# Handling of the samples' columns and the written order of VectorE and ScalarE in the RMS norms of a five-stage transformer step

## The chip, the cores and the metric

The kernel runs on one core of a Trainium2 chip. A core has TensorE (PE in the profile, PEld for its weight loads), VectorE (DVE), ScalarE (ACT), GpSimd (POOL) and SyncE (SP, which only issues transfers). The metric is the device time of one launch in microseconds. All arithmetic is fp32 in and out; the matrix products use pairs of rounded values (hi and lo), as told below.

## What is computed

The reference takes 1024 prompt columns and 64 sample columns (8 sequences of 8 tokens) of 1024 features. Four stages run one after the other: attention (stage 0), a gated MLP (stage 1), an RWKV mixing layer (stage 2) and another MLP (stage 3), then a last norm. Each stage starts with an RMS norm whose output is modulated:

```
r  = 1 / sqrt(mean(x*x over features) + eps)
h  = x * r * scale[stage] + shift[stage]
x  = x + gate[stage] * block(h)
```

The factors scale, shift and gate belong to a condition: the prompt has one condition for all its columns, and each of the 8 sample sequences has its own. So for the prompt they are one number a feature, for the samples 8 numbers a feature.

## The kernel before

Features lie on the partitions: x is eight tiles f = 0 to 7 of 128 features. The 1088 columns are worked in two halves: A has 576 prompt columns (products in chunks of 288), B has 448 prompt columns and the 64 samples (one chunk of 512). So the samples are columns 448 to 511 of a B half; an A half has none. Each half runs each stage's norm, so there are ten norms with the last ones.

A norm has three steps. `rms` (L246) squares x on ScalarE (sq, L253), sums over partitions by TensorE (ssq, L255), takes a square root on ScalarE (rv, L259), refines it in six VectorE operations (L260 to L265), spreads the result over all partitions by four TensorE products, one for each quarter of the columns (rb, L269), and copies them alternately by ScalarE (L120) and VectorE (L122) into R. `norm_split` (L294) then makes for each f the modulated tile hf and its rounded parts hhi and hlo: for the prompt, VectorE multiplies (L279), ScalarE adds the shift and rounds (L304), VectorE takes the rest (L305). For the samples `modulate` has POOL multiply by R (L283), by the scales (L284) and add the shifts (L285), ScalarE rounds (cast, L120) and POOL takes the rest (L292). `rw_norm` does the same for stage 2, where the modulated tile is kept (h) and mixed with its neighbour column (x, L828) before it is split into xhi and xlo.

`dense` (L329) runs over output tiles m. For each it loads a weight tile (wst), which `weight` (L313) rounds to wh on ScalarE (L323), the rest wl half on POOL (L325) and half on VectorE (L326). Then for each f it multiplies wh·hi (L339), wh·lo (L340) and wl·hi (L341) into one output tile dq. Three such tiles can be open at a time, so TensorE uses each hi and lo part up to three times before it has to wait for the next f. `residual` (L345) takes dq back into x: for the prompt one VectorE operation (L354); for the samples VectorE multiplies by the gates (rs, L357) and POOL adds (L360).

Other work runs beside the dense products: attention (softmax-like scans L529, products with the running result L530) beside stages 0 and 1, RWKV's chains (S, L1137; lane work tm and lxn, L1191 and L1193; qc, L1300 and on) beside stages 1 to 3. Code order gives each engine's instructions only loosely: a scheduler at build time decides by its own costs the order in which each engine runs them, and on the chip every engine keeps to that order and waits where an operand is late. Weight transfers are issued on SP (L320).

Of the kernel before, what the change touches and what calls it, by code (L numbers as in the profile page):

```python
# [10 lines left out]
F32 = mybir.dt.float32  # L11
# [44 lines left out]
SLOT = 576  # L56


C_ID, C_SEL9, C_SELB, C_MN, C_M64, C_M8, C_BLK, C_B8 = 0, 128, 144, 656, 664, 792, 920, 1048
C_H16, C_SELN, C_MQ, C_MQ1, C_MN1 = 1056, 1072, 1200, 1264, 1328  # L60
C_N = 1336


def make_consts():
    c = np.zeros((128, C_N), np.float32)
    p = np.arange(128)
    c[:, C_ID:C_ID + 128] = np.eye(128)
    for v in range(9):
        c[p % 32 == v, C_SEL9 + v] = 1.0
    for g in range(4):  # L70
        c[32 * g, C_SELB + 128 * g:C_SELB + 128 * (g + 1)] = 1.0
    for t in range(8):
        c[p % 8 > t, C_MN + t] = 1.0
    s = (p % 64)[:, None]
    t = np.arange(64)[None, :]
    c[:, C_M64:C_M64 + 64] = s < t
    c[:, C_M64 + 64:C_M64 + 128] = s <= t
    same = (s // 8) == (t // 8)
    c[:, C_M8:C_M8 + 64] = (s < t) & same
    c[:, C_M8 + 64:C_M8 + 128] = (s <= t) & same  # L80
    c[:64, C_BLK:C_BLK + 64] = 1.0
    c[64:, C_BLK + 64:C_BLK + 128] = 1.0
    for b in range(8):
        c[(p % 64) // 8 == b, C_B8 + b] = 1.0
    for h in range(16):
        c[p // 8 == h, C_H16 + h] = 1.0
    c[:, C_MQ:C_MQ + 64] = t < s
    c[:, C_MQ1:C_MQ1 + 64] = t >= s
    c[:, C_MN1:C_MN1 + 8] = 1.0 - c[:, C_MN:C_MN + 8]
    c[p % 32 == 0, C_SELN:C_SELN + 64] = 1.0  # L90
    c[p % 32 == 16, C_SELN + 64:C_SELN + 128] = 1.0
    return c


class Kern:
# [35 lines left out]
    def setup(self, ctx):  # L131
# [12 lines left out]
        self.beside(iter(()), 0.0)  # L144
        self.eps = self.misc.tile([128, 1], F32, name="eps")
        nc.vector.memset(self.eps, EPS)

    def load_params(self):

# [96 lines left out]
    def rms(self, x, pt, tmp, ps, tag, slot, rslot=None):  # L246

        nc = self.nc
        W, w = pt.W, pt.W // 4
        q = ps.tile([128, 512], F32, tag=tag, name="ssq")  # L250
        for f in range(NT):
            sq = tmp.tile([128, W], F32, tag=slot, name="sq")
            nc.scalar.activation(sq, x[f], AF.Square)  # L253
# [12 lines left out]
        R = tmp.tile([128, W], F32, tag=rslot or slot, name="R", bufs=2 if rslot else None)  # L266
        for g in range(4):
            qb = ps.tile([128, 512], F32, tag=tag, name="rb")
            nc.tensor.matmul(qb[:, :w], self.cst[:, C_SELB + 128 * g:C_SELB + 128 * g + 128], r,  # L269
                             start=True, stop=True)  # L270
            self.copy(R[:, w * g:w * g + w], qb[:, :w])
        return R

    def modulate(self, s, f, x, R, pt, t):

        nc = self.nc
        mod = self.mod[s]
        P, S = slice(0, pt.NP), slice(pt.NP, pt.W)
        nc.vector.scalar_tensor_tensor(t[:, P], x[f][:, P], mod[:, 8 + f, 0:1], R[:, P], ALU.mult,  # L279
                                       ALU.mult)  # L280
        if pt.NP < pt.W:
            ts = t[:, S].rearrange("p (b t) -> p b t", b=8)
            nc.gpsimd.tensor_mul(t[:, S], x[f][:, S], R[:, S])  # L283
            nc.gpsimd.tensor_mul(ts, ts, mod[:, 8 + f, 1:9].unsqueeze(2).to_broadcast([128, 8, 8]))  # L284
            nc.gpsimd.tensor_add(ts, ts, mod[:, f, 1:9].unsqueeze(2).to_broadcast([128, 8, 8]))  # L285
        return mod[:, f, 0:1]

    def split(self, src, hi, lo, heng="a", leng="v"):
        nc = self.nc
# [4 lines left out]
    def norm_split(self, s, x, R, pt, pool, tmp, slot):  # L294

        nc = self.nc
        hi, lo = [], []
        P, S = slice(0, pt.NP), slice(pt.NP, pt.W)
        for f in range(NT):
            t = tmp.tile([128, pt.W], F32, tag=slot, name="hf")  # L300
            B = self.modulate(s, f, x, R, pt, t)
            a = pool.tile([128, pt.W], F32R, tag="h", name="hhi")
            b = pool.tile([128, pt.W], F32R, tag="h", name="hlo")
            nc.scalar.activation(a[:, P], t[:, P], AF.Identity, bias=B)  # L304
            nc.vector.scalar_tensor_tensor(b[:, P], t[:, P], B, a[:, P].bitcast(F32), ALU.add,  # L305
                                           ALU.subtract)
            if pt.NP < pt.W:
                self.split(t[:, S], a[:, S], b[:, S], "a", "g")
            hi.append(a)
            lo.append(b)  # L310
        return hi, lo


# [31 lines left out]
    def residual(self, s, x, pt, tmp):  # L345
# [4 lines left out]
        def evac(m, c0, n, q):  # L350
# [4 lines left out]
            if np_ < n:  # L355
# [1 line left out]
                nc.vector.tensor_mul(t, q[:, np_:n].rearrange("p (b t) -> p b t", b=8),  # L357
                                     mod[:, 16 + m, 1:9].unsqueeze(2).to_broadcast([128, 8, 8]))
                xv = x[m][:, pt.NP:].rearrange("p (b t) -> p b t", b=8)
                nc.gpsimd.tensor_add(xv, xv, t)  # L360
        return evac


# [495 lines left out]
    def rw_norm(self, x, R, pt, pool, tmp):  # L859
# [2 lines left out]
        e = 1 if pt.o else 0  # L862
        W = pt.W
        hi, lo, hs = [], [], []

        def mixed(f):
            t = tmp.tile([128, W], F32, tag="n", name="x")
# [5 lines left out]
        for f in range(NT):  # L873
# [4 lines left out]
                nc.gpsimd.tensor_copy(he[:, 0:1], self.hl[:, f:f + 1])  # L878
            B = self.modulate(2, f, x, R, pt, h)
            nc.scalar.activation(h[:, :pt.NP], h[:, :pt.NP], AF.Identity, bias=B)  # L880
            if not e:
                nc.gpsimd.tensor_copy(self.hl[:, f:f + 1], h[:, W - 1:W])
            nc.sync.dma_start(self.hscr[f][:, pt.cols], h)
# [877 lines left out]
```

## Time and profile before

| | before |
|---|---|
| median of 3 runs | 3700.04 us (3698.4 to 3703.11) |
| profiled execution | 3712.77 us, its span 3710.8 us |
| TensorE busy | 3497.1 us, 94% |
| VectorE / ScalarE / POOL busy | 63% / 43% / 33% |
| mean granted TensorE clock | 0.962 |

The columns of a timeline row are: start, length, engine, line, operation, output and input, count, and in brackets the engine's idle time before it with what ended it. A waits row has total us, times and the longest. A group of a tile has the shortest, median and longest duration in ns. The profiled execution is 12.7 us longer than the median, so a sum worked out in it is applied as a difference.

### The profile page before, as it was taken

To read this page: it belongs to the slowest core of one execution; us is meant where nothing else is said; L and a number is where in the kernel's file an instruction comes from. 1 tells how busy PE (TensorE), PEld (TensorE's weight loads), DVE (VectorE), ACT (ScalarE), POOL (GpSimd) and SP (SyncE) were. 2 spreads that over 40 slices of the span, in tenths; PEclk is the share of its full clock that TensorE was granted. 3 is DMA by queue.
4 is the path that set the end of the run, shared out by engine and by line. 5 is a ranking of instruction groups with operands and counts; after the bars stand their busy time and mean duration, and the time that the engine had idled before them with its cause. 6 is when DMAs were issued, how large, how long until landed. Compare 5 with 4: busy or idle time off the path is not lost.

```text
span 3710.8 us, 72191 instructions
## 1 busy us (share of the span) xinstructions
PE 3497.1 (94%) x26360; PEld 2785.7 (75%) x26360; DVE 2320.9 (63%) x4718; ACT 1594.7 (43%) x3342; POOL 1235.3 (33%) x1692
## 2 busy tenths in 40 slices
PE   8999999899999999988799998998899999989998
PEld 5786767688888877766677776656698888877887
DVE  4246778996555556687846556666884666645444
ACT  3145666764333345634334445543433344332232
POOL 1136544443222222223423234223221222243332
PEclk9999999999999999988899998998899999989999
DMA  8845444125989885666254445557344444333332
GB/s 303 278 153 185 155 132 114 46 74 201 333 318 346 310 315 163 198 202 202 80 148 138 122 146 160 192 175 228 115 134 132 143 140 139 99 113 111 97 94 83
DMA packets 431860, 632.43 MB, mean 170 GB/s; under 512 B 144209, under 2 KB 244434, under 8 KB 431506
## 3 DMA queue, kind: packets, MB, share of 16 engines
q1 hardware_dynamic: 368242, 530.80, 44.5%
q10 hardware_dynamic: 63264, 97.02, 7.8%
q8 instruction: 209, 3.42, 0.4%
q14 instruction: 145, 1.19, 0.1%
HBM read 521.66 MB, written 106.01 MB: 169 GB/s over the span
## 4 chain that ended last, share of the span: by engine, by line
PE 40%; DVE 7%; DMA 3%; issue 2%; POOL 1%; ACT 1%; SPq 1%; ACTq 0%; DVEq 0%; POOLq 0%
PE dq L339 11%; PE dq L340 11%; PE dq L341 10%; DVE lxn L1193 1%; DVE tm L1191 1%; PE qc L1310 1%; PE qc L1300 1%; PE qc L1319 1%; PE yq L1467 1%; PE bonq L1459 0%; PE qc L1314 0%; PE invq L1260 0%; DMA s_v<-vt 0%; DVE wl L326 0%; PE qc L1323 0%
## 5 line engine op out<-in xcount | busy, mean ns | idle before, releaser
L325 POOL TENSOR_TENSOR wl<-wst,wh 128x256 fp32r<-128x256 f32 (+1 forms) x512 | 648.0, 1267 | 1580.3 <-ACT wh L323 1367.6
L323 ACT CAST wh<-wst 128x512 fp32r<-128x512 f32 (+1 forms) x512 | 424.7, 834 | 747.2 <-PE dq L340 589.9
L339 PE MATMUL dq<-hhi,wh 128*128 128x288 f32 (+1 forms) x2112 | 712.7, 338 | 31.2 <-ACT hhi L120 24.5
L340 PE MATMUL dq<-hlo,wh 128*128 128x288 f32 (+1 forms) x2112 | 709.0, 336 | 3.3 <-POOL prod L525 1.4
L341 PE MATMUL dq<-hhi,wl 128*128 128x288 f32 (+1 forms) x2112 | 704.6, 334 | 1.5 <-POOL wl L325 1.5
L326 DVE TENSOR_TENSOR wl<-wst,wh 128x256 fp32r<-128x256 f32 (+1 forms) x512 | 353.8, 694 | 264.6 <-ACT wh L323 226.2
L339 PE MATMUL dq<-uh,wh 128*128 128x288 f32 (+1 forms) x1536 | 505.7, 334 | 4.0 <-DVE rs L357 1.7
L340 PE MATMUL dq<-ul,wh 128*128 128x288 f32 (+1 forms) x1536 | 507.2, 331 | 0.0
L341 PE MATMUL dq<-uh,wl 128*128 128x288 f32 (+1 forms) x1536 | 505.3, 332 | 0.0
L339 PEld LDWEIGHTS dq<-hhi,wh 128*128 128x128 f32 x2112 | 402.8, 191 | 78.1 <-ACT hhi L120 25.5
L340 PEld LDWEIGHTS dq<-hlo,wh 128*128 128x128 f32 x2112 | 402.1, 190 | 51.0 <-issue 14.7
L341 PEld LDWEIGHTS dq<-hhi,wl 128*128 128x128 f32 x2112 | 401.7, 190 | 45.3 <-issue 14.5
L354 DVE SCALAR_TENSOR_TENSOR x<-dq,mod,x 128x288 f32<-128x288 f32 (+1 forms) x432 | 245.3, 569 | 269.9 <-PE dq L341 267.3
L339 PEld LDWEIGHTS dq<-uh,wh 128*128 128x128 f32 x1536 | 287.7, 188 | 43.5 <-issue 11.7
L529 DVE TENSOR_TENSOR_SCAN prod<-prod 128x256 f32<-128x256 f32 (+5 forms) x264 | 247.4, 938 | 104.9 <-ACT prod L520 65.3
L340 PEld LDWEIGHTS dq<-ul,wh 128*128 128x128 f32 x1536 | 288.4, 188 | 30.6 <-issue 9.2
L341 PEld LDWEIGHTS dq<-uh,wl 128*128 128x128 f32 x1536 | 288.1, 188 | 29.5 <-issue 7.0
L339 PE MATMUL dq<-xhi,wh 128*128 128x288 f32 (+1 forms) x576 | 206.4, 359 | 2.6 <-DVE gt L122 1.1
L340 PE MATMUL dq<-xlo,wh 128*128 128x288 f32 (+1 forms) x576 | 201.8, 350 | 3.0 <-POOL xlo L292 1.6
L341 PE MATMUL dq<-xhi,wl 128*128 128x288 f32 (+1 forms) x576 | 199.2, 346 | 0.0
L451 DVE TENSOR_TENSOR ut<-ut 128x288 f32<-128x288 f32 (+1 forms) x192 | 153.1, 798 | 40.5 <-ACT ut L450 37.8
L453 ACT CAST uh<-ut 128x288 fp32r<-128x288 f32 (+1 forms) x192 | 95.2, 496 | 189.2 <-DVE ut L451 186.8
(300 smaller groups left out, 6296.6 us busy)
## 6 DMA issues: line engine op xcount, KB each, us to landing
pagek<-cache_kT SPq DMA_DIRECT2D x128, 512.0 KB
pagev<-cache_v SPq DMA_DIRECT2D x128, 512.0 KB
adaw<-ada_w SPq DMA_DIRECT2D x192, 256.0 KB
wst<-w_up SPq DMA_DIRECT2D x96, 512.0 KB
wst<-w_down SPq DMA_DIRECT2D x192, 256.0 KB
st<-s_st SPq DMA_DIRECT2D x40, 672.0 KB
wst<-sb_w_qkv SPq DMA_DIRECT2D x48, 512.0 KB
wst<-w_up ACTq DMA_DIRECT2D x32, 512.0 KB
```

The lines of the kernel that those rows point to most:

```text
L323: nc.scalar.copy(wh, st)
L325: nc.gpsimd.tensor_sub(wl[:, :h], st[:, :h], wh[:, :h].bitcast(F32))
L326: nc.vector.tensor_sub(wl[:, h:], st[:, h:], wh[:, h:].bitcast(F32))
L339: nc.tensor.matmul(q, wh[:, k, :], h, start=k == 0, stop=False)
L340: nc.tensor.matmul(q, wh[:, k, :], l, start=False, stop=False)
L341: nc.tensor.matmul(q, wl[:, k, :], h, start=False, stop=k == kt - 1)
L354: nc.vector.scalar_tensor_tensor(xs, q[:, :np_], g, xs, ALU.mult, ALU.add)
L451: nc.vector.tensor_mul(t[:, :n], t[:, :n], t[:, :n])
L453: nc.scalar.copy(a, t[:, :n])
L529: nc.vector.tensor_tensor_scan(r, r, r, 1.0 if carry is None else carry, ALU.mult, ALU.bypass)
L1191: eng.tensor_mul(t, lt[P, s, s + 1:32].unsqueeze(2).to_broadcast([N, a, c]), xn[P, s, 0:c].unsqueeze(1).to_broadcast([N, a, c]))
L1193: eng.tensor_add(xn[P, s + 1:32, 0:c], xn[P, s + 1:32, 0:c], t)
```

## The change

Five edits.

1. The samples of all eight f are modulated together on VectorE: `modulate_samples` makes one tile hs (128 x 8 x 64), by eight multiplications with R and then one multiplication and one addition over all 512 values, with scales and shifts broadcast. ScalarE still rounds them; VectorE takes the rest (L314 of the new kernel).
2. The samples' residual add moves from POOL to VectorE (L380).
3. The four rb products use only 32 rows each, the row group in which the quarter's result stands (`self.R4[g]`), and the table of constants is smaller by 384 columns.
4. `rms` begins with a square root of a small tile into a tile `warm`.
5. `norm_split` runs under a manual schedule for VectorE and ScalarE: their instructions keep the order written there, hf0, hf1, lo0, hf2, lo1 and so on. Other work may still be put between them.

```diff
+        nc.scalar.activation(self.warm, self.eps, AF.Sqrt)
...
-            nc.tensor.matmul(qb[:, :w], self.cst[:, C_SELB + 128 * g:C_SELB + 128 * g + 128], r,
-                             start=True, stop=True)
+            rows = self.R4[g]
+            nc.tensor.matmul(qb[:, :w], self.cst[rows, C_SELB:C_SELB + 128], r[rows], start=True,
+                             stop=True)
...
-        if pt.NP < pt.W:
-            ts = t[:, S].rearrange("p (b t) -> p b t", b=8)
-            nc.gpsimd.tensor_mul(t[:, S], x[f][:, S], R[:, S])
-            nc.gpsimd.tensor_mul(ts, ts, mod[:, 8 + f, 1:9].unsqueeze(2).to_broadcast([128, 8, 8]))
-            nc.gpsimd.tensor_add(ts, ts, mod[:, f, 1:9].unsqueeze(2).to_broadcast([128, 8, 8]))
...
+    def modulate_samples(self, s, x, R, pt, tmp, slot):
+
+        nc = self.nc
+        mod = self.mod[s]
+        S = slice(pt.NP, pt.W)
+        t = tmp.tile([128, NT, TS], F32, tag=slot, name="hs")
+        for f in range(NT):
+            nc.vector.tensor_mul(t[:, f, :], x[f][:, S], R[:, S])
+        v = t.rearrange("p f (b t) -> p f b t", b=8)
+        for op, j in ((ALU.mult, 8), (ALU.add, 0)):
+            nc.vector.tensor_tensor(v, v, mod[:, j:j + NT, 1:9].unsqueeze(3).to_broadcast(
+                [128, NT, 8, 8]), op)
+        return t
...
+        def lower(f, B):
+            nc.vector.scalar_tensor_tensor(lo[f][:, P], ts[f][:, P], B, hi[f][:, P].bitcast(F32),
+                                           ALU.add, ALU.subtract)
             if pt.NP < pt.W:
-                self.split(t[:, S], a[:, S], b[:, S], "a", "g")
+                nc.vector.tensor_sub(lo[f][:, S], hs[:, f, :], hi[f][:, S].bitcast(F32))
+        with self.tc.manual_schedule(engines={mybir.EngineType.DVE, mybir.EngineType.Activation}):
+            if pt.NP < pt.W:
+                hs = self.modulate_samples(s, x, R, pt, tmp, slot)
+            last = None
+            for f in range(NT):
...
+                nc.scalar.activation(hi[f][:, P], ts[f][:, P], AF.Identity, bias=B)
+                if pt.NP < pt.W:
+                    nc.scalar.copy(hi[f][:, S], hs[:, f, :])
+                if last:
+                    lower(*last)
+                last = f, B
+            lower(*last)
...
-                nc.gpsimd.tensor_add(xv, xv, t)
+                nc.vector.tensor_add(xv, xv, t)
```

In `rw_norm` the samples' h is likewise copied by ScalarE out of an hs tile. The new kernel's line numbers are 1 higher in `rms` and about 20 higher behind `norm_split`.

What this does to the order of the instructions is shown at three places. The first is VectorE at the norm of stage 3's B half, before (x, dq, rs: the residual; ssq, rv, R: the norm; mod: the table of scales, shifts and gates):

```order
L357 TENSOR_TENSOR rs<-dq,mod_1507 128x64
L326 TENSOR_TENSOR wl<-wst,wh 128x512
L260 TENSOR_SCALAR rv<-ssq 128x128
...
L122 COPY R<-rb 128x128 x2
L279 SCALAR_TENSOR_TENSOR hf<-x,mod_3223,R 128x448 x6
L305 SCALAR_TENSOR_TENSOR hlo<-hf,mod_3223,hhi 128x448 x5
L279 SCALAR_TENSOR_TENSOR hf<-x,mod_3223,R 128x448 x2
L305 SCALAR_TENSOR_TENSOR hlo<-hf,mod_3223,hhi 128x448 x3
```

and in the changed kernel:

```order
L377 TENSOR_TENSOR rs<-dq,mod_1513 128x64
L346 TENSOR_TENSOR wl<-wst,wh 128x512
L380 TENSOR_TENSOR x<-x,rs 128x64
L261 TENSOR_SCALAR rv<-ssq 128x128
...
L121 COPY R<-rb 128x128 x2
L291 TENSOR_TENSOR hs<-x,R 128x64 x8
L294 TENSOR_TENSOR hs<-hs,mod_3219 128x512 x2
L280 SCALAR_TENSOR_TENSOR hf<-x,mod_3219,R 128x448 x2
L311 SCALAR_TENSOR_TENSOR hlo<-hf,mod_3219,hhi 128x448
L314 TENSOR_TENSOR hlo<-hs,hhi 128x64
L280 SCALAR_TENSOR_TENSOR hf<-x,mod_3219,R 128x448
```

The residual add and ten operations on hs are new on this engine, and each lo follows the next f's hf, where six hf ran ahead of the first lo.

The second is VectorE at the same norm of stage 1, where RWKV's lane operations (tm, lxn) stand beside it. Before:

```order
L357 TENSOR_TENSOR rs<-dq,mod_179 128x64
L326 TENSOR_TENSOR wl<-wst,wh 128x512
L1137 TENSOR_TENSOR S<-s_20900,cst 64x192
...
L265 TENSOR_TENSOR rv<-rv 128x128
L1191 TENSOR_TENSOR tm<-llt,lxn 72x31
L122 COPY R<-rb 128x128
...
L122 COPY R<-rb 128x128
L1191 TENSOR_TENSOR tm<-llt,lxn 72x87
L279 SCALAR_TENSOR_TENSOR hf<-x,mod_828,R 128x448 x3
L1193 TENSOR_TENSOR lxn<-lxn,tm 72x29x3
L279 SCALAR_TENSOR_TENSOR hf<-x,mod_828,R 128x448 x3
```

and in the changed kernel:

```order
L377 TENSOR_TENSOR rs<-dq,mod_181 128x64
L1215 TENSOR_TENSOR tm<-llt,lxn 72x112
L346 TENSOR_TENSOR wl<-wst,wh 128x512
L380 TENSOR_TENSOR x<-x,rs 128x64
...
L266 TENSOR_TENSOR rv<-rv 128x128
L1215 TENSOR_TENSOR tm<-llt,lxn 72x207
...
L291 TENSOR_TENSOR hs<-x,R 128x64 x5
L1215 TENSOR_TENSOR tm<-llt,lxn 72x240
L291 TENSOR_TENSOR hs<-x,R 128x64 x3
L1217 TENSOR_TENSOR lxn<-lxn,tm 72x20x12
L294 TENSOR_TENSOR hs<-hs,mod_834 128x512
```

The twelve S operations between the last residual and rv have gone ahead of the residual, with the TensorE products that they feed, and lane operations stand between the steps of the norm instead.

The third is ScalarE's start, in the changed kernel:

```order
L251 ACT_TABLE_LOAD
L251 ACTIVATE warm<-eps 128x1 x10
L164 ACT_TABLE_LOAD
L164 ACTIVATE cs<-c 128x72
L254 ACTIVATE sq<-x 128x576 x8
L260 ACT_TABLE_LOAD
L260 ACTIVATE rv<-ssq,eps 128x144
```

All ten warm-up square roots, one written at each norm, stand ahead of the first operation of the program, and the first norm still has a table load before its square root. At stage 1's A half (mixed with attention), the stretch of VectorE from the first hf to the last lo holds 11 rows of attention before and 25 in the changed kernel: 10 scans (5 before), 9 products L550 (5), two copies (1) and four casts (none).

More of the change, by code (lines that the diff above doesn't have):

```diff
@@ L69, in make_consts @@
         c[p % 32 == v, C_SEL9 + v] = 1.0
-    for g in range(4):
-        c[32 * g, C_SELB + 128 * g:C_SELB + 128 * (g + 1)] = 1.0
+    c[p % 32 == 0, C_SELB:C_SELB + 128] = 1.0
     for t in range(8):
@@ L146, in setup @@
         nc.vector.memset(self.eps, EPS)
+        self.warm = self.misc.tile([128, 1], F32, name="warm")
     def load_params(self):
```

34 lines of the change are left out of this document (16 added, 18 removed).

## The prediction

> **What bounds the kernel now.** I read the share of busy time first, then the list of waits, and then the timeline around each norm. The page's first part:
>
> ```profile
> PE 3497.1 (94%) x26360; PEld 2785.7 (75%) x26360; DVE 2320.9 (63%) x4718; ACT 1594.7 (43%) x3342; POOL 1235.3 (33%) x1692
> ```
>
> TensorE is busy for 94% of the span, so an edit pays only where TensorE stands still. The change touches no matmul of the dense products; it can only shorten the stalls of TensorE around the ten norms, or lengthen them. The waits that name its lines (total us, times, longest):
>
> ```profile
> ACT sq L253 <- POOL x L360: 41.5, 22, 5.0
> PE dq L339 <- ACT hhi L120: 24.5, 3, 10.5
> ```
>
> The second row is the target: three times, once in each norm_split of a B half, TensorE waits for the cast of the samples' columns, 24.5 us together. The first is ScalarE waiting for the add of the samples; ScalarE is 43% busy, and this matters only where squares of a norm are the last thing TensorE waits for. The norm of stage 3's B half shows the chain whole:
>
> ```profile
> 3312.01 0.69 DVE L354 SCALAR_TENSOR_TENSOR x<-dq,mod,x 128x448 f32<-128x448 f32 x1 [3.85 <-PE dq L341]
> 3312.61 0.21 DVE L357 TENSOR_TENSOR rs<-dq,mod 128x64 f32<-128x64 f32 x1
> 3312.90 0.69 DVE L326 TENSOR_TENSOR wl<-wst,wh 128x512 fp32r<-128x512 f32 x1
> 3313.00 1.72 POOL L325 TENSOR_TENSOR wl<-wst,wh 128x512 fp32r<-128x512 f32 x1 [3.41 <-ACT wh L323]
> 3314.68 0.31 POOL L360 TENSOR_TENSOR x<-x,rs 128x64 f32<-128x64 f32 x1
> 3315.03 0.63 ACT L253 ACTIVATE sq<-x 128x512 f32<-128x512 f32 x1 [1.62 <-POOL x L360]
> ...
> 3319.21 2.04 PE L269 MATMUL rb<-rv,cst 128*128 128x128 f32 x8 [2.98 <-DVE rv L265]
> ...
> 3321.29 0.29 DVE L122 COPY R<-rb 128x128 f32<-128x128 f32 x1 [0.56 <-PE rb L269]
> 3321.66 3.61 POOL L283 TENSOR_TENSOR hf<-x,R 128x64 f32<-128x64 f32 x6 [6.67 <-DVE R L122]
> 3321.69 4.07 DVE L279 SCALAR_TENSOR_TENSOR hf<-x,mod,R 128x448 f32<-128x448 f32 x6
> 3322.50 2.64 ACT L304 ACTIVATE hhi<-hf,mod 128x448 fp32r<-128x448 f32 x4 [1.37 <-DVE hf L279]
> 3325.24 3.47 POOL L284 TENSOR_TENSOR hf<-hf,mod 128x64 f32<-128x64 f32 x6
> 3328.67 2.01 POOL L285 TENSOR_TENSOR hf<-hf,mod 128x64 f32<-128x64 f32 x6
> 3328.99 0.24 ACT L120 CAST hhi<-hf 128x64 fp32r<-128x64 f32 x1 [3.85 <-POOL hf L285]
> ...
> 3329.29 0.80 PE L339 MATMUL dq<-hhi,wh 128*128 128x512 f32 x1 [8.03 <-ACT hhi L120]
> 3331.01 0.79 PE L340 MATMUL dq<-hlo,wh 128*128 128x512 f32 x1 [0.93 <-POOL hlo L292]
> ```
>
> R is complete at 3321.58. The prompt's first hi part is there 1.6 us later, yet the first product starts at 3329.29, because POOL runs all its first multiplications, then all second ones, and only then an addition that a cast can use. The groups of the tile hf (duration in ns: shortest, median, longest):
>
> ```profile
> L305 DVE SCALAR_TENSOR_TENSOR hlo<-hf,mod,hhi x48: 653/786/873, 24.2 to 3335.8; 128x576 fp32r<-128x576 f32 x24, 128x448 fp32r<-128x448 f32 x24
> L283 POOL TENSOR_TENSOR hf<-x,R x24: 309/695/4675, 280.9 to 3333.2; 128x64 f32<-128x64 f32 x24
> L284 POOL TENSOR_TENSOR hf<-hf,mod x24: 288/382/942, 284.0 to 3334.3; 128x64 f32<-128x64 f32 x24
> L285 POOL TENSOR_TENSOR hf<-hf,mod x24: 284/290/2307, 287.1 to 3334.8; 128x64 f32<-128x64 f32 x24
> ```
>
> The profiled execution took 3712.77 us, 12.7 above the median of 3700.04. My sum is a difference worked out inside the profiled execution; I take it from the median.
>
> **Norm of stage 3, B half.** Removed: the add on POOL behind its 1.72-us weight part. On DVE the add stands behind L326, which ends at 3313.59; at about the 0.21 us of L357 it is done at 3313.8, not 3314.99: −1.2. From there to R nothing changes but the four rb matmuls, now on 32 rows each. No row has this form. They cost at most the 2.04 us they take now; four copies on two engines (0.29 each) follow in any case, so the gain is 0 to 0.8, and I take 0.5. R is then complete at about 3319.9. Next on DVE come eight 128x64 multiplications at 0.2 (the 0.21 of L357) and two 128x512 operations at 0.69 (L326), 3.0 us; the first hf of 0.68 (4.07/6), its hi of 0.66 (2.64/4) and the cast of 0.24: the first product at about 3324.5, not 3329.29, −4.8. The lo parts follow on DVE, 0.65 and 0.2 each, faster than TensorE asks, so the 0.93 wait for POOL's lo goes too. Some of this returns later, since stage 3's first weights and the final norm of the A half follow. I take **−5**, bounds −7 to −2.
>
> **Norm of stage 1, B half.** Same chain, with RWKV lane work in it:
>
> ```profile
> 1788.00:1814.00 26.00, 8.41 (x75) 6.45 (x76) 16.00 (x42) 9.83 (x23) 10.46 (x18) 0.61 0.36 108
> ```
>
> This row is a window: PE, PEld, DVE, ACT, POOL busy. TensorE works 8.41 of 26 us.
>
> ```profile
> 1788.76 0.65 DVE L354 SCALAR_TENSOR_TENSOR x<-dq,mod,x 128x448 f32<-128x448 f32 x1
> ...
> 1796.84 1.28 ACT L259 ACT_TABLE_LOAD   x1
> 1798.13 0.37 ACT L259 ACTIVATE rv<-ssq,eps 128x128 f32<-128x128 f32 x1
> ...
> 1802.95 0.19 DVE L1191 TENSOR_TENSOR tm<-llt,lxn 72x31 f32<-72x31 f32 x1 [2.03 <-DMA llt<-s_l]
> ...
> 1803.88 0.28 DVE L122 COPY R<-rb 128x128 f32<-128x128 f32 x1
> ...
> 1804.23 7.21 POOL L283 TENSOR_TENSOR hf<-x,R 128x64 f32<-128x64 f32 x6 [13.92 <-DVE R L122]
> ...
> 1813.55 1.65 PE L339 MATMUL dq<-hhi,wh 128*128 128x512 f32 x3 [10.50 <-ACT hhi L120]
> ```
>
> One multiplication took 4675 ns here (the group's longest). The new order has DVE after the last residual as x, rs, wl, add (2.0 us with one lane operation), then four lane operations, rv, R, hs, hf, with ten more lane operations in the rv chain and three in hs. At 0.3 us each (0.19 at 31 elements a lane, growing to 255) I get: ssq and sqrt about 5 us after x begins, rv with its lane work 3.9, rb and R about 2 to 3 with lane work, hs 3.0 plus 1.0, hf, hi and cast 1.6: about 16 to 17 us, against the 24.8 from 1788.76 to 1813.55. But the 5 to 6 us of TensorE work that fill this window now (8.41 less about 2 for rb, as in stage 3, and about 1 for the squares' sums) stand ahead of the last residual in the new order and cover nothing here. Net −8 + 5.5 plus the wait for the chain at its head, which is no longer the norm's: between −9 and +4; I take **−4.5**, nearer the gain because a POOL stall of 10.50 us has a row and the lost cover is work that must run anyway.
>
> **Norms of stage 0's B half, RWKV's B half, and the last.**
>
> ```profile
> 289.69 1.22 PE L339 MATMUL dq<-hhi,wh 128*128 128x512 f32 x2 [5.93 <-ACT hhi L120]
> ...
> 2293.87 0.45 PE L1300 MATMUL qc<-hv,st 128*64 128x64 f32 x2 [2.28 <-ACT x L828]
> ...
> 3696.03 0.32 POOL L360 TENSOR_TENSOR x<-x,rs 128x64 f32<-128x64 f32 x1 [2.39 <-DVE rs L357]
> ```
>
> In the first, a POOL addition of 2307 ns (the group's longest) goes, and 3.0 us of hs come ahead of the first hf on DVE, which shares it with attention's scans: **−1.7** (−4 to +2, the wait of 5.93 being the most there is). In RWKV's the stall is 2.28 and hs costs DVE 3.0 before the first h: **−1** (−2.3 to +2). In the last norm POOL's add starts right behind rs, so moving it saves 0.1, and rb up to 1: **−0.6** (−1.5 to 0).
>
> **Norm of stage 1, A half.** It has no samples; only the written order acts. DVE is full of attention's scans there:
>
> ```profile
> 709.94 2.34 DVE L279 SCALAR_TENSOR_TENSOR hf<-x,mod,R 128x576 f32<-128x576 f32 x3 [0.33 <-ACT R L120]
> ...
> 728.32 0.81 DVE L305 SCALAR_TENSOR_TENSOR hlo<-hf,mod,hhi 128x576 fp32r<-128x576 f32 x1
> L529 DVE TENSOR_TENSOR_SCAN prod<-prod 128x256 f32<-128x256 f32 (+5 forms) x264 | 247.4, 938 | 104.9 <-ACT prod L520 65.3
> ```
>
> From the first hf to the end of the last lo it takes 19.2 us. The new order puts 14 more attention rows into that stretch (five scans at 0.94, nine smaller ones at about half): 9 us, so the last lo comes after some 28 us. TensorE gets attention's products earlier in exchange; between 0 and +9, and I take **+3**, a third, since the attention rows release matmuls of their own.
>
> **The early table load.** The order shows that it doesn't do what it says: all ten warm-up activations stand at ScalarE's start, and the square roots that had a table load of their own in five norms still have one. The start pays: one more load (1.28 as above) and ten tiny activations, in front of
>
> ```profile
> 5.04 0.26 ACT L164 ACTIVATE cs<-c 128x72 f32<-128x72 f32 x1 [2.94 <-DMA c<-c]
> ```
>
> whose 2.94 us wait for a DMA covers most: 1.28 and 10 x 0.2 less 2.94 is **+0.3** (−0.5, with a smaller table of constants to load, to +1). In a sentence apart: the Trainium skill, "ScalarE: Activation LUTs", What ACT_TABLE_LOAD costs, states 1283 ns and about 1380 ns of drain, 2.66 us a switch; the load here agrees with 1.28, but the sqrt follows 0.01 us behind it, so five loads hidden would be worth 6.4 us by the rows and 13.3 by the page.
>
> **What is added elsewhere.** 144 residual adds at 0.2, hs at 3.0 in four B halves and 24 lo parts at 0.2 put some 46 us on DVE, which is 63% busy under a 94% busy TensorE: nothing, save where DVE is full, and there (stage 1's norms) it is counted. By the Trainium skill, "SBUF — State Buffer", Who interferes with whom, a DVE operation with two SBUF inputs shuts out a GpSimd operation that reads SBUF; the 4675 ns against a shortest 309 agrees. By that rule these 46 us would lengthen POOL's weight parts by as much, on an engine 33% busy, which leaves the sum alone. All other rows shift a little, since the order is decided anew: 0, bounds −6 to +6.
>
> Sum: −5 − 4.5 − 1.7 − 1 − 0.6 + 3 + 0.3 = −9.5. From 3700.04 this gives **3690.5 us**, its own range 3680 to 3700.
>
> **The rivals.**
>
> *No change.* What the norms win is given back by the new order: the lost cover in stage 1's B half makes that term 0, stage 1's A half costs 6, the rest −8: 3698. For it: two of the biggest terms have bounds of both signs; against it: stage 3's B half has nothing beside it on DVE.
>
> *Slower.* The written order, one mechanism: DVE and ScalarE can no longer take a late hi or lo out of turn, so a lo of the prompt stands behind hs, lane or scan rows while TensorE has used up its three output tiles. The place is stage 1, both halves: +9 for A (all of the 9 us) and +4 for B, and +2 each in stage 0's and RWKV's B halves; with −5 − 0.6 + 0.3 that is +11.7: 3712. It decides from where the two stage-1 terms together exceed +8. Against it: a lo of 0.65 to 0.87 us is far shorter than what TensorE does with one part, nine products over its three output tiles at some 0.5 (the 1.65 of the row of three).
>
> *The POOL waits weigh more.* All upper gains, −7 − 9 − 4 − 2.3 − 1.5, and A at 0: 3676. For it: the 41.5 us of ScalarE's waits for POOL's add; against: ScalarE has time.
>
> **How the numbers follow.** Forecast 0.5, no change 0.27, slower 0.16, larger gain 0.07. A measurement of this kernel tells about 0.2%, 7.4 us, from no change: faster means below 3692.6. Of the forecast's 0.5, some 0.36 lies below that bound and 0.14 within; of no change 0.03 is faster, 0.21 same and 0.03 slower. Faster 0.46, same 0.36, slower 0.18. The range reaches from within the larger gain to within the slower rival: 3675 to 3708.
>
> **What would show it.** In stage 3's B half the first dq should start some 13 us after the last residual's x (17.3 now), with no POOL row between; in stage 1's the 10.50-us wait should be under 8 and named after ScalarE's cast of a DVE tile; the ACT table load must still stand ahead of stage 1's sqrt; the last lo of stage 1's A half should lie 26 to 29 us behind its first hf. The forecast falls if TensorE's waits for lo parts grow in stage 1 by more than the norms win, or if the sums of waits around the norms fall by 9 us and the time doesn't.

## The result, and the profile after

The changed kernel takes 3729.68 us (five runs, 3721.10 to 3735.42), the kernel before 3701.44 on the same chip: ratio 1.0063, 95% interval 1.0047 to 1.0079. (A ratio and its interval are estimated over all the runs, so they can differ a little from the quotient of the two medians, here 1.0076.) By the medians it is slower by 28 us where 9.5 us less were forecast; even the upper end of the range, 3708, lies below it.

Three of the norms did much of what was forecast. The list of waits of the changed kernel (total us, times, longest):

```profile
PE dq L359 <- ACT hhi L326: 9.8, 2, 5.4
ACT sq L254 <- DVE x L380: 38.5, 18, 7.5
```

The first row was 24.5 us before, the second 41.5 (for POOL's add). So some 15 us of the wait for the cast are gone. Waits for a lo part have partly come in their place: 6.2 us in nine, against 1.8 in two before. Some 10 us are left of it, and the kernel still lost. The first part of its page says where not to look:

```profile
PE 3502.9 (94%) x26360; PEld 2788.2 (75%) x26360; DVE 2384.2 (64%) x4926; ACT 1594.5 (43%) x3357; POOL 1132.9 (30%) x1428
```

VectorE has 63 us more work and is still at 64%. TensorE runs the same 26360 instructions; they take 5.8 us longer (3502.9 against 3497.1), and the span less TensorE's busy time, its idle time, is 222.9 us against 213.7, 9.2 more in spite of the shorter waits in the norms. This profiled execution is 15 us longer than the one of before, about half of what the medians differ by, so the sums below are of one execution each.

The norm of stage 3's B half, timeline of the changed kernel:

```profile
3327.82 0.68 DVE L374 SCALAR_TENSOR_TENSOR x<-dq,mod,x 128x448 f32<-128x448 f32 x1 [2.62 <-PE dq L361]
3328.42 0.21 DVE L377 TENSOR_TENSOR rs<-dq,mod 128x64 f32<-128x64 f32 x1
...
3328.76 1.77 POOL L345 TENSOR_TENSOR wl<-wst,wh 128x512 fp32r<-128x512 f32 x1 [3.64 <-ACT wh L343]
3329.33 1.29 DVE L380 TENSOR_TENSOR x<-x,rs 128x64 f32<-128x64 f32 x1
...
3330.71 0.63 ACT L254 ACTIVATE sq<-x 128x512 f32<-128x512 f32 x1 [1.49 <-DVE x L380]
...
3334.82 0.81 PE L271 MATMUL rb<-rv,cst 32*128 32x128 f32 x6 [3.00 <-DVE rv L266]
...
3335.93 0.79 PE L271 MATMUL rb<-rv,cst 32*128 32x128 f32 x2 [0.31 <-ACT R L119]
3336.76 0.29 DVE L121 COPY R<-rb 128x128 f32<-128x128 f32 x1 [0.81 <-PE rb L271]
3337.09 1.17 DVE L291 TENSOR_TENSOR hs<-x,R 128x64 f32<-128x64 f32 x8
3338.29 1.42 DVE L294 TENSOR_TENSOR hs<-hs,mod 128x512 f32<-128x512 f32 x2
...
3341.20 0.80 PE L359 MATMUL dq<-hhi,wh 128*128 128x512 f32 x1 [4.47 <-ACT hhi L326]
3341.92 0.80 PE L360 MATMUL dq<-hlo,wh 128*128 128x512 f32 x1
```

From the last residual's x to the first product it is 13.4 us, where it was 17.3 and 13 was forecast; no POOL row of the norm stands in between, and the wait of 0.93 us before the first lo is gone. One row is not as forecast: the residual add took 1.29 us, not 0.21, beside POOL's 1.77-us weight part. In stage 1's B half

```profile
1814.67 0.68 DVE L374 SCALAR_TENSOR_TENSOR x<-dq,mod,x 128x448 f32<-128x448 f32 x1
...
1818.21 1.28 ACT L260 ACT_TABLE_LOAD   x1
...
1830.18 1.65 PE L359 MATMUL dq<-hhi,wh 128*128 128x512 f32 x3 [5.36 <-ACT hhi L326]
```

the wait is 5.36 us (10.50 before), the way from x to the first product 15.5 us (24.8; 16 to 17 forecast), and the table load still stands ahead of the square root. The loss lies elsewhere. Summed over TensorE's products in order (counted by the 4608 products wh·lo), the changed kernel has 4.8 us less idle time than before behind the first 192, 0.8 more behind 1920, 9.5 more behind 2304 and 15.6 more behind 2689. The stretch from 1920 to 2304 holds the norm just shown, which won, so what lies around it lost more than that. Two of its longest waits are these, in stage 2's products:

```profile
1698.90 0.61 PE L359 MATMUL dq<-xhi,wh 128*128 128x288 f32 x1 [5.80 <-ACT vt L119]
...
1734.92 0.90 PE L127 MATMUL vq<-cst,dn 128*128 128x128 f32 x3 [6.57 <-DVE dn L121]
```

Neither names a line of the change. Both are RWKV's products, which the change does not touch but whose places among the dense products the build has chosen anew. The kernel before has such waits too (one of 10.57 us at 1692.40, before an RWKV product), so it is the sum that shows the loss, not a single row. The last 6 us of the 15.6 come at RWKV's norm of the B half, which is taken up below.

### The profile page after: what moved, and what is told of

The parts are those of the page before. It is cut to its first block, busy times and chain, and to the rows that moved or that the text cites. A ratio compares the mean times of both kernels' runs of the same rounds, so it can differ in the third digit from the quotient of the medians.

```text
span 3725.8 us, 72104 instructions
## 1 busy us (share of the span) xinstructions
PE 3502.9 (94%) x26360; PEld 2788.2 (75%) x26360; DVE 2384.2 (64%) x4926; ACT 1594.5 (43%) x3357; POOL 1132.9 (30%) x1428
## 4 chain that ended last, share of the span: by engine, by line
PE 74%; DVE 13%; DMA 5%; issue 3%; ACT 3%; POOL 1%; SPq 1%; ACTq 1%; DVEq 0%; POOLq 0%
PE dq L359 19%; PE dq L361 18%; PE dq L360 18%; PE tq L127 2%; PE o L618 2%; PE zs L682 2%; PE os L740 2%; PE adaq L234 2%; DVE prod L549 1%; PE z L584 1%; PE qc L1334 1%; PE qc L1324 1%; PE qc L1343 1%; DVE wl L346 1%; DVE tm L1215 1%
## 5 line engine op out<-in xcount | busy, mean ns | idle before, releaser
L345 POOL TENSOR_TENSOR wl<-wst,wh 128x256 fp32r<-128x256 f32 (+1 forms) x512 | 652.0, 1276 | 1652.7 <-ACT wh L343 1479.2
L360 PEld LDWEIGHTS dq<-hlo,wh 128*128 128x128 f32 x2112 | 402.1, 190 | 53.3 <-issue 11.2
L359 PE MATMUL dq<-xhi,wh 128*128 128x288 f32 (+1 forms) x576 | 205.9, 358 | 13.6 <-ACT vt L119 5.8
```

The lines of the kernel that those rows point to most:

```text
L345: nc.gpsimd.tensor_sub(wl[:, :h], st[:, :h], wh[:, :h].bitcast(F32))
L359: nc.tensor.matmul(q, wh[:, k, :], h, start=k == 0, stop=False)
L360: nc.tensor.matmul(q, wh[:, k, :], l, start=False, stop=False)
```

## Experiments

Three theories were tested first. O: any edit makes the build deal out the background work anew, and that order, not the edit's work, sets the difference. Against it stood W (the written order costs) and V (VectorE has too much to do). All ratios are to the kernel before on the same chip; its medians were 3701 to 3709 us.

| | what runs | median us | ratio | 95% interval |
|---|---|---|---|---|
| the change | five edits | 3729.68 | 1.0063 | 1.0047 to 1.0079 |
| e1 | written order alone | 3739.53 | 1.0095 | 1.0071 to 1.0119 |
| e2 | samples on VectorE alone | 3729.50 | 1.0070 | 1.0047 to 1.0094 |
| e3 | residual add alone | 3707.30 | 1.0003 | 0.9987 to 1.0018 |
| e4 | 32-row products alone | 3739.52 | 1.0097 | 1.0073 to 1.0121 |
| e5 | e4's work, old order | 3708.75 | 1.0002 | 0.9990 to 1.0015 |
| e6 | old work, e4's order | 3738.66 | 1.0085 | 1.0059 to 1.0111 |
| e7 | edits 1 to 3, old order (hf and lo of the B norms in the written order) | 3701.51 | 0.9988 | 0.9975 to 1.0002 |
| e8 | warm-up alone | 3710.99 | 1.0009 | 0.9993 to 1.0024 |
| e9 | old work, the change's TensorE order | 3749.86 | 1.0116 | 1.0091 to 1.0140 |
| e10 | five edits, old TensorE order | 3724.50 | 1.0042 | 1.0023 to 1.0060 |
| e11 | written order in stage 1's A half, old order | 3708.60 | 1.0004 | 0.9988 to 1.0020 |
| e12 | e7 with hs in two pieces | 3705.15 | 0.9997 | 0.9986 to 1.0009 |
| e13 | e10, RWKV's samples on POOL | 3718.08 | 1.0026 | 1.0010 to 1.0041 |
| e14 | e10 without the written order | 3738.61 | 1.0082 | 1.0060 to 1.0105 |

### Single edits (e1 to e4)

e1 takes the new norm_split with its manual schedule and leaves the samples where they were:

```diff
+        with self.tc.manual_schedule(engines={mybir.EngineType.DVE, mybir.EngineType.Activation}):
...
+                nc.gpsimd.tensor_sub(lo[f][:, S], ts[f][:, S], hi[f][:, S].bitcast(F32))
```

> The kernel before with edit 5 alone: norm_split in the written order hf0, hf1, lo0, ... under the manual schedule for VectorE and ScalarE, samples and residual add still on POOL. Theory W (the written order costs): the 28 us of the change come with it, 3720 or more, with TensorE's waits for lo parts grown in stage 1. Theory V (VectorE has too much): within 5 us of 3701. Theory O (the order of the background work is dealt anew by any edit, and that, not the edit's own work, sets most of the difference): anywhere from 3690 to 3730, with the norms' own waits about as before and the loss in stages 1 and 2 away from norms.

e2 adds `modulate_samples` as in the change, without the manual schedule.

> The kernel before with edit 1 alone: hs on VectorE, no manual schedule. Theory W: the norms' waits for the cast shorten by some 10 us and nothing else changes, 3690 to 3696. Theory V: the 12 us of VectorE work in four norms cost, 3705 or more. Theory O: the waits for the cast shorten by some 10 us, and the time lies anywhere from 3685 to 3720, by stalls in RWKV's stage.

e3 changes one line:

```diff
-                nc.gpsimd.tensor_add(xv, xv, t)
+                nc.vector.tensor_add(xv, xv, t)
```

> The kernel before with edit 2 alone: the samples' residual add on VectorE. Theory W: 3700, at most 2 us less. Theory V: 144 adds of 0.2 us, 29 us of VectorE work beside RWKV's chains, cost up to that: 3715 to 3725. Theory O: 3690 to 3720, with no wait of TensorE that names the add.

e4 changes the rb products and the table of constants:

```diff
-            nc.tensor.matmul(qb[:, :w], self.cst[:, C_SELB + 128 * g:C_SELB + 128 * g + 128], r,
+            rows = self.R4[g]
+            nc.tensor.matmul(qb[:, :w], self.cst[rows, C_SELB:C_SELB + 128], r[rows], start=True,
```

> The kernel before with edit 3 alone: the rb products on 32 rows each, the smaller table of constants. Its own work is worth 0 to 1 us in each of ten norms. Theories W and V: 3693 to 3701. Theory O: its order of the background is dealt anew as well, so the time may differ by 5 to 20 us in either direction, though the work is less.

Measured: +33.5, +23.5, +1.3 and +33.5 us. Three of the four lie beyond what O had allowed (up to 3730, up to 3720, and 5 to 20 us). e4 is the telling one. It takes work out and adds none, and it loses 33.5 us. V falls with e3, which puts 144 operations on VectorE (2380.1 us busy, 59 of the change's 63 us more) and loses nothing measurable.

e1 and e2 also tell which edit shortens the wait for the cast, and it is not the one that the prediction credited. Stage 3's B half in e1, where the samples are still on POOL:

```profile
3347.92 1.64 POOL L283 TENSOR_TENSOR hf<-x,R 128x64 f32<-128x64 f32 x3 [6.83 <-DVE R L122]
3349.52 1.67 POOL L284 TENSOR_TENSOR hf<-hf,mod 128x64 f32<-128x64 f32 x3
3351.15 0.80 POOL L285 TENSOR_TENSOR hf<-hf,mod 128x64 f32<-128x64 f32 x3
...
3351.77 0.79 PE L347 MATMUL dq<-hhi,wh 128*128 128x512 f32 x1 [4.26 <-ACT hhi L314]
```

and in e2, where they are on VectorE without the written order:

```profile
3341.03 3.06 DVE L278 SCALAR_TENSOR_TENSOR hf<-x,mod,R 128x448 f32<-128x448 f32 x5
...
3344.01 0.68 DVE L292 TENSOR_TENSOR hs<-hs,mod 128x512 f32<-128x512 f32 x1
3344.61 2.46 DVE L309 SCALAR_TENSOR_TENSOR hlo<-hf,mod,hhi 128x448 fp32r<-128x448 f32 x4
3346.99 0.68 DVE L292 TENSOR_TENSOR hs<-hs,mod 128x512 f32<-128x512 f32 x1
...
3348.01 0.79 PE L357 MATMUL dq<-hhi,wh 128*128 128x512 f32 x1 [8.43 <-ACT hhi L324]
```

Before, the wait was 8.03 us, in the change 4.47. With the written order POOL runs three operations of a kind where it ran six, and the wait is as short as in the change; without it the second hs operation stands behind five hf and four lo, and nothing is won. Stage 1's B half agrees (5.15 us in e1, 11.14 in e2, 10.50 before, 5.36 in the change). But e1 then waits longer for lo parts. The waits for the cast and for lo together are 26.3 us before, 22.4 in e1 (9.4 and 13.0), 23.6 in e2 (19.6 and 4.0) and 16.0 in the change: each edit alone wins little here, both together some 10 us.

e4's page, and its mean granted clock:

```profile
PE 3512.4 (94%) x26360; PEld 2796.9 (75%) x26360; DVE 2323.5 (62%) x4718; ACT 1594.8 (43%) x3342; POOL 1240.6 (33%) x1692
```

```profile
core 0: 3736.1 us, clock 0.955
```

TensorE's idle time is 223.7 us, 10.0 more than before; and the same 26360 instructions take 15.3 us longer than the 3497.1 of before, at a mean granted clock of 0.955 instead of 0.962. So in this execution the loss has two parts, idle time and products that take longer at a lower mean clock. That is not a rule for every stall: e2, e10 and e14 have 18.3, 13.6 and 16.7 us more idle time than the kernel before, and their busy time is not longer (3496.1, 3494.7 and 3494.7 us). Why e4's products also lost clock stays open.

### The order against the work (e5, e6)

In these two, each engine's instructions are tied one behind the other in a given order, which is read from a table:

```diff
         Kern(tc, I, O).run()
+        pin(nc, tc)
...
+        for a, b in zip(o[:-1], o[1:]):
+            tc.add_manual_dep(mine[e][b], mine[e][a].name, mybir.DependencyInfo(
+                mybir.DependencyClass.NoSync, mybir.DependencyReason.DATA), reason="order")
```

The built order of e5 is that of the kernel before, row for row, and the built order of e6 that of e4.

> The work of the kernel with the 32-row rb products alone, but every engine's instructions held to the order they have in the kernel before (each tied behind the one ahead of it on its engine). Theory O (the order costs, not the work): the 33 us that this edit lost are gone, 3695 to 3706. Rival P (the 32-row products are slow themselves, or what follows them): 3735 or more again.

> The mirror image: the work of the kernel before, to the last operand, held to the order that the 32-row edit's build gave each engine. Theory O: 3735 to 3745 with nothing of the computation changed, TensorE's added idle time at the end of RWKV's stage and the start of stage 3. Rival P: 3700 to 3706.

Measured: e5 3708.75 against 3707.79 us, e6 3738.66. The work of e4 in the old order loses nothing measurable; the untouched work in e4's order loses 31 us. This shows O for e4. The page of e6:

```profile
PE 3505.7 (94%) x26360; PEld 2797.8 (75%) x26360; DVE 2321.5 (62%) x4718; ACT 1596.2 (43%) x3342; POOL 1246.4 (33%) x1692
```

Idle time is 226.4 us (12.7 more than before), busy time 8.6 more. What such an order does can be seen at the norm of stage 3's A half. ScalarE and TensorE in e6 (ACTq is ScalarE's transfer queue):

```profile
2671.11 2.72 ACTq L1162 DMA_DIRECT2D s_st<-S  x2
2673.86 1.28 ACT L1068 ACT_TABLE_LOAD   x1 [3.77 <-DMA s_st<-S]
...
2676.31 0.46 ACT L120 COPY R<-rb 128x144 f32<-128x144 f32 x2
...
2678.93 1.51 ACT L304 ACTIVATE hhi<-hf,mod 128x576 fp32r<-128x576 f32 x2
```

```profile
2679.76 1.09 PE L339 MATMUL dq<-hhi,wh 128*128 128x288 f32 x3 [8.01 <-ACT hhi L304]
```

and ScalarE in the kernel before:

```profile
2654.66 0.28 ACT L120 COPY R<-rb 128x144 f32<-128x144 f32 x1 [5.41 <-PE rb L269]
2655.62 0.28 ACT L120 COPY R<-rb 128x144 f32<-128x144 f32 x1 [0.68 <-PE rb L269]
...
2660.44 1.50 ACT L304 ACTIVATE hhi<-hf,mod 128x576 fp32r<-128x576 f32 x2 [2.16 <-DVE hf L279]
```

Before, ScalarE stood idle until rb came and copied R at once. In e6 RWKV's transfers, a table load and the activations behind it stand ahead of the R copies on ScalarE's queue; ScalarE waits 3.77 us for them, R and then hhi come late, and TensorE waits 8.01 us. No row of it is slow; they stand in another sequence. This place is one of several: counted at the wh·lo products (4608 in all), e6 has at the 2688th 9.2 us less idle time on TensorE behind it than the kernel before, at the 2880th 3.8 us more, and at the end 12.7 more.

### The edits in the old order (e7, e8, e12)

e7 puts edits 1 to 3 and, in the three B norms, the written order of edit 5 into the old order. The TensorE order is the old one row for row. hs stands ahead of hf0, the residual add right behind rs, and hf and lo of the three B norms take their old places in the written order. RWKV's norm keeps its samples on POOL.

> Edits 1 to 3 (the samples in norm_split's three B halves and the residual add on VectorE, 32-row rb products) put into the order of the kernel before: TensorE's order is its order row for row, the removed POOL operations are left out, the new VectorE operations stand right behind what they need, and within the three B norms hf and lo take their old places in the written order. RWKV's norm keeps its samples on POOL, and there is no warm-up. Theory O: the norms' own wins show, 5 to 12 us: 3688 to 3700. Rival V (VectorE's extra 40 us cost by themselves): 3706 or more.

Measured 3701.51 against 3707.79 us, 0.9988, interval up to 1.0002. The loss is gone, V falls again (VectorE's extra work is all here but for RWKV's norm), and what is left of the win can't be told from nothing. Its page and its wait for the cast:

```profile
PE 3510.0 (94%) x26360; PEld 2789.7 (75%) x26360; DVE 2393.3 (64%) x4916; ACT 1593.7 (43%) x3342; POOL 1099.3 (30%) x1452
```

```profile
PE dq L356 <- ACT hhi L324: 11.2, 3, 5.9
```

Idle time is 205.1 us in a span of 3715.1, 8.6 less than before; the prediction's terms for these norms come to 11.8 (−5, −4.5, −1.7 and −0.6). But TensorE's busy time is 12.9 us more, so this execution, the slowest of its ten, won nothing. One execution's idle time is also a loose measure: e8 and e11, which change next to nothing, have 216.7 and 208.4 us against the 213.7 of before. e12 makes hs in two pieces, so that the first product waits for two f instead of eight:

```diff
-        for f in range(NT):
-            nc.vector.tensor_mul(t[:, f, :], x[f][:, S], R[:, S])
+        for f0, n in ((0, 2), (2, NT - 2)):
+            for f in range(f0, f0 + n):
+                nc.vector.tensor_mul(t[:, f, :], x[f][:, S], R[:, S])
```

> Edits 1 to 3 in the order of the kernel before, with hs made in two pieces: the first two f before hf0, the other six behind lo0. The first product of each of three B norms then waits for 1.1 us of hs instead of 3.0. Expected from e7's waits of 5.91 and 4.47 us: some 2 us less at each, 4 to 6 us below e7: 3692 to 3700, and faster than the kernel before by 0.2 to 0.4%. If the clock gives back what the waits save: 3700 to 3706.

Its wait for the cast fell from 11.2 to 7.2 us, about as expected, but it brought nothing measurable, 0.9997, and the 3705.15 us lie where the expectation had put them if the clock gives the gain back. Its idle time is 203.6 us (span 3707.0 less 3503.4 busy), 10.1 less than before, and busy time 6.3 more. The runs of the kernel before show how far the time moves by itself: over 25 runs of one batch its time ranged from 3694.98 at a mean clock of 0.970 to 3720.00 at 0.958. Mean clocks over all runs were 0.9637 (before, 25 runs), 0.9625 (e7, 10) and 0.9620 (e12, 12). Whether the shorter stalls cost clock or this is chance stays open. No version beat the kernel before measurably.

e8 is the warm-up alone; every other row of its built order is the old one.

> The kernel before with edit 4 alone. Its build leaves every engine's order as it was but for the ten warm-up activations and one table load at ScalarE's start. Theory O: no measurable difference, 3698 to 3708. Rival: the table loads around the norms are moved off the chain, 3693 to 3697.

Measured 1.0009, 0.9993 to 1.0024: no difference, as its place at the start of the program lets expect.

### The change's own order (e9, e10)

TensorE's products are the same 20824 in both kernels, so their order can be exchanged; the build chooses the other engines' orders around it, so these two runs do not hold everything else fixed as e5 and e6 do.

> The work of the kernel before; only TensorE's order is held to the one of the changed kernel (its products are the same 20824, one for one), and the other engines' orders are chosen by the build around it. Theory O: the loss of the change comes with TensorE's order: 3720 to 3738. Rival (the loss sits in the changed kernel's own VectorE and ScalarE work): 3700 to 3710.

> All five edits, with TensorE's order held to the one of the kernel before and the other engines' orders chosen by the build around it. Theory O: the loss is gone and the norms' own win remains: 3692 to 3708. Rival: 3720 to 3735 again.

Measured +43 us for e9: the old work in the change's TensorE order is slower than the change itself. e9's page (span 3749.9, so 241.2 us idle, 27.5 more than before):

```profile
PE 3508.7 (94%) x26360; PEld 2797.0 (75%) x26360; DVE 2313.5 (62%) x4718; ACT 1591.5 (42%) x3338; POOL 1246.3 (33%) x1692
```

So this TensorE order, with the orders that the build gives the other engines around it, accounts for the whole loss and more; with the edits in it, the change, it loses some 15 us less. e10 at +18 us is better than the change but not free of loss; O alone had it at 3708 at most. Its rows at RWKV's norm of the B half show one cause:

```profile
2287.14 0.29 DVE L121 COPY R<-rb 128x128 f32<-128x128 f32 x1
...
2295.05 0.68 DVE L294 TENSOR_TENSOR hs<-hs,mod 128x512 f32<-128x512 f32 x1
...
2297.53 0.80 DVE L294 TENSOR_TENSOR hs<-hs,mod 128x512 f32<-128x512 f32 x1
...
2304.00 0.80 PE L359 MATMUL dq<-xhi,wh 128*128 128x512 f32 x1 [7.18 <-ACT xhi L119]
```

R is complete at 2287.4, the last hs operation 10.9 us later, with rows of RWKV's chain between (rw_norm is not under the manual schedule), and no f can go on before all eight are done.

### What remains in e10 (e11, e13, e14)

e11 puts only the sixteen hf and lo operations of stage 1's A half into the written order; in four of the sixteen places this exchanges an hf and a lo.

> The kernel before in its own order on every engine, except that in the norm of stage 1's A half VectorE's sixteen hf and lo operations take their places in the written order hf0, hf1, lo0, hf2, and so on; nothing is put between them that wasn't there. The prediction's term of +3 (bounds 0 to +9) came from this place, two thirds or more of it from attention rows placed between. Expected: within 4 us of 3705. If the written order itself starves TensorE there: 3709 or more.

Measured 1.0004, 0.9988 to 1.0020: nothing measurable. e13 gives RWKV's norm its POOL operations back, in the old TensorE order; e14 takes the manual schedule out of e10:

```diff
-        with self.tc.manual_schedule(engines={mybir.EngineType.DVE, mybir.EngineType.Activation}):
+        if True:
```

> The five edits in TensorE's old order (as e10), but RWKV's norm keeps its samples on POOL. In e10 the first dense product of that norm waited 7.18 us for its cast, since the second hs operation stood behind RWKV's own work on VectorE and ended 10.9 us after R. Theory R (the part of the loss that TensorE's order doesn't explain comes from hs in that norm): 7 us or more below e10's 3724.5, 3708 to 3717, with TensorE's idle time between 2192 and 2306 us back to what it was before. Rival (it is spread over VectorE's other moved rows): 3720 to 3728.

> The five edits in TensorE's old order (as e10), without the manual schedule of edit 5. Theory R: 3720 to 3728, since hs in RWKV's norm is still there. Theory S (the written order in the norms of stages 1 and 3 costs the rest, its waits for lo of up to 2.9 us): 3710 to 3718.

e13: 3718.08, 6 us below e10, with overlapping intervals, between what the two expectations had; but the wait of 7.18 us is gone from its trace. The other 9 us over the kernel before are open: e13's profiled execution, at 3708.5 us, was one of its fastest and doesn't show them. e14: 3738.61, 14 us above e10 and beyond both expectations, so W has the wrong sign here. Its wait for the cast:

```profile
PE dq L359 <- ACT hhi L326: 30.4, 3, 11.6
```

In e10 that row is 15.2 us, before the change 24.5. Without the written order the hs operations lie apart: in stage 3's B half the second stands behind five hf and four lo as in e2 (a wait of 8.43 us again), in stage 0's also behind attention's scans (11.6), in stage 1's also behind RWKV's lane work (10.4). The profiled execution of e14 was its fastest and is only 3.1 us longer than e10's, so these rows show 15 us more wait for the cast, but not where the 14 us of the medians lie.

## Why the prediction was wrong

**The step that failed** is the sentence "All other rows shift a little, since the order is decided anew: 0, bounds −6 to +6". That term was taken as small noise around zero. With the work of the kernel before and only the order changed it is +31 us for e4's order (e6) and +43 us for the change's TensorE order (e9), and four single edits gave +33.5, +23.5, +1.3 and +33.5. It is not noise around zero either: none of the new orders that were timed was measurably faster than the old one.

**What bounds the kernel now.** "An edit pays only where TensorE stands still" holds, but it was applied to the ten norms alone. TensorE's order also decides how long it waits for RWKV's chains, and these waits name no line of the change.

**The norms.** Their lengths came near the forecast, but not for the reason given. The prediction credited the move of the samples from POOL to VectorE; e1 and e2 show that this move alone shortens no wait for the cast in stages 1 and 3, that the written order alone does (to 5.15 and 4.26 us), and that the move then saves waits for lo. The prediction priced the written order only as a cost, though its sum for these norms has hs ahead of the first hf, as that order puts it. Stage 3's B half: the wait fell by 3.56 us and the 0.93 for lo went; 13.4 us from x to the first product against some 13 forecast. TensorE's idle time on this way fell from 12.9 to 9.5 us, 3.4 where 5 was taken, with bounds 2 and 7. Within it one part failed: the add on VectorE was to save 1.2 us and saved 0.1, since it took 1.29 beside POOL's weight part (sq starts 2.89 us after x; 3.02 before). Rb and its copies were to save 0.5 and saved 0.1 (2.23 us from rb's start to the end of R, 2.37 before), since the last rb waits for ScalarE's copy of an earlier one, 0.31. From R to the first product it takes 4.15 us (4.6 forecast, 7.71 before): this is where the win is. Stage 1's B half: 5.36 us under the forecast bound of 8. The way is 9.3 us shorter, and 4.1 us of products that filled it no longer do (7.96 us of TensorE's work before, 3.85 now; 5.5 was counted as lost), so the idle time fell by 5.2, with −4.5 forecast. In stage 0's B half the wait of 5.93 us for the cast is gone; one of 1.62 for a lo and one of 2.92 for attention stand there now. In the last norm the add and rb saved nothing: from the last add's start to R it takes 6.75 us, 6.25 before. Together the idle time that e7 saves, 8.6 us, is not far from the 11.8 of these terms; that it turns into time was taken for granted and isn't shown.

**RWKV's norm**, taken as −1 (to +2), cost some 6 us in e10 (e13 is 6 us faster without it, with overlapping intervals): the sum counted hs as 3.0 us of work, not as 3.0 us cut into pieces by other rows. In the changed kernel itself the last hs operation ended 7.5 us after R:

```profile
2334.42 0.29 DVE L121 COPY R<-rb 128x128 f32<-128x128 f32 x1
...
2341.50 0.68 DVE L294 TENSOR_TENSOR hs<-hs,mod 128x512 f32<-128x512 f32 x1
...
2348.97 0.79 PE L359 MATMUL dq<-xhi,wh 128*128 128x512 f32 x1 [3.30 <-ACT xhi L119]
```

**Stage 1's A half** was taken as +3 (0 to +9). The first hf, TensorE's longest wait for a lo, and the last lo:

```profile
715.48 1.55 DVE L280 SCALAR_TENSOR_TENSOR hf<-x,mod,R 128x576 f32<-128x576 f32 x2 [0.29 <-ACT R L119]
...
743.19 0.40 PE L360 MATMUL dq<-hlo,wh 128*128 128x288 f32 x1 [2.33 <-DVE hlo L311]
...
746.39 0.82 DVE L311 SCALAR_TENSOR_TENSOR hlo<-hf,mod,hhi 128x576 fp32r<-128x576 f32 x1
```

It is 31.7 us from the first hf to the end of the last lo, where 26 to 29 were forecast and 19.2 stood before. TensorE waits three times for a lo there, 3.0 us together, and did not before. That this equals the +3 is luck: the term was a third of 9 us, and the stretch grew by 12.5. The exchange of hf and lo itself costs nothing measurable there (e11); what the rows placed between cost was not measured apart.

**The early table load** and **VectorE's extra work** were right in that neither has a measurable effect (e8, e3). The extra work was sized too small: VectorE is busy 63 us more, not 46, mainly since the 144 adds took 80.0 us and not 0.2 each (e3, with the adds alone, has 59 us more). The prediction reckoned with POOL's weight parts becoming longer by as much as VectorE's new work; they took 652.0 us in all, 648.0 before, and it was VectorE's adds that waited.

**The rivals.** The time lies beyond the slower one, 3712, and its mechanism isn't the main one found: its waits for a late lo do appear in stage 1's A half, 3.0 us, but the written order, which it blamed, also makes the samples' edit worth having (e1, e2, e14). "No change" named the new order as what gives the wins back, with 3698; it had the right cause at far too small a size.

## What to carry to other kernels

Where a build decides the order of background work anew, a change's worth can't be read from its own instructions: hold the old order (or exchange the orders of the two kernels) and time the work and the order apart. Here the five new TensorE orders (the change's and those of e1 to e4), each with its edit in it, cost between 0 and 1.0%, the change's own with the old work 1.2%; so price a new order from a few edits that do nearly nothing before pricing the edit. Work that is put together for one reader pays only if it is also kept together in its engine's queue. And where edits come together, time each alone: here the wait fell by the written order, not by the faster engine.

## What the runs showed of the hardware

A small VectorE operation can be held up by a GpSimd one. The residual add (the group of the changed kernel with shortest, median and longest in ns, then with its busy time in us, mean in ns and the idle time ahead of it):

```profile
L380 DVE TENSOR_TENSOR x<-x,rs x144: 157/222/1322, 1759.8 to 3710.3; 128x64 f32<-128x64 f32 x144
L380 DVE TENSOR_TENSOR x<-x,rs 128x64 f32<-128x64 f32 x144 | 80.0, 556 | 0.8
```

41 of the 144 took over 1 us; each of these ran beside one of POOL's weight parts and ended within 0.1 us of it (in stage 3's last residual the add's 1.29 us ended at 3330.62, POOL's 1.77 us at 3330.53). The Trainium skill, "SBUF — State Buffer", Who interferes with whom, has both directions: a VectorE operation with two SBUF inputs and a GpSimd operation that reads SBUF exclude each other. The long adds agree with it. The prediction weighed it only for what POOL would lose.

The run-to-run scatter of one kernel goes with the granted clock: the ends of the 25 runs above, 25.0 us and 0.012 of clock apart, make about 2 us for each 0.001, and a line through all 25 gives 1.8. The Trainium skill, "TensorE: Matmul & The Clock Gate", What's actually happening, calls the window that sets the clock free-running and its effect variable from run to run; the runs agree in that they vary; that the window runs free is shown by no run here. The same page puts the ramp's price below 1% of a typical span; here the scatter alone is 0.7% of the time, nearly as large as what the change lost.
